# Nine of eleven pairs of rows of an FFN's last projection as block products, their weight sums in groups of three

## The chip, the cores and the metric

The kernel runs on one core of a Trainium2 chip. The metric is the device time of one execution in microseconds (us). The engines are named as in the profile: PE is TensorE (matmuls; PEld its weight loads), DVE is VectorE, ACT is ScalarE, POOL is GpSimd and SP is SyncE, which here only issues transfers. Times inside an execution are counted from the start of the profiled span.

## The reference

One layer of a streaming encoder on x of 512 tokens by 1024 features: a normalization, a combined input projection, banded attention beside a gated linear recurrence, both merged by gates and a projection, and then a gated FFN. All in float32. The part that the change touches is the last product:

```python
h = h + (g_a * ya + g_b * yb) @ w_o[l]
hn = rmsnorm(h, norm_ffn_g[l])
gu = hn @ w_ffn_in[l]
g, up = jnp.split(gu, 2, axis=-1)
h = h + (jax.nn.silu(g) * up) @ w_ffn_out[l]
return rmsnorm(h, final_norm_g)
```

`w_ffn_out` has 2816 rows and 1024 columns: 22 blocks of 128 rows, or eleven pairs of blocks, 512 KB for each half of the columns.

## The kernel before

Every float32 operand of a matmul is split into a high part (ACT rounds it by a copy, L86) and a low part (DVE subtracts, L87). One product of a 128x128 operand with 512 columns is then three matmuls, high by high, high by low and low by high (`mm3`, L78).

**Two ways to do a pair.** Let a pair be the 512 tokens by 256 inner features of the activation, times 256 rows by 1024 columns of `w_ffn_out`. A *plain* pair (`out_pair`, L1527) multiplies each of four token blocks with each of two halves of the columns, over two row blocks: 4 x 2 x 2 x 3 = 48 matmuls of 512 columns. A *block* pair cuts the activation and the weights into 2 x 2 blocks and does seven block products instead of eight (`out_block`, L1533): 7 x 2 x 3 = 42 matmuls. For that it needs sums. On the activation's side `a_first` (L1507) splits the left operand of the first products, `a_sums` (L1511) makes four sums with DVE and splits them into the right operand, and `a_second` and `a_last` (L1521, L1524) make the left and right operands of the later products. On the weights' side it needs t1 to t4, which are sums of the four blocks of the weights. The results of the seven products are added to and subtracted from the rows of `h` out of PSUM (`h_add`, L1537; `h_sum`, L1541).

**The weight sums** are made in DRAM while earlier stages run. Pairs are put in groups of `GROUP` (L206). For each group and kind SP copies a block of the weights into a buffer (`out_copy`, L222), and POOL then adds another one to it by an accumulating transfer (`out_add`, L226). All copies and sums are kept in a list each, t1 and t3 of every group first, then t2, then t4. `step` (L238) takes the next one from a list. Copies are taken one after each of the 16 attention heads, as `COPIES` says (L1166). Sums are taken after the heads in `ADDS_AT`, then one beside each of the first four products of the attention's output projection (L1186, the tiles `po_ya`), and then in the FFN's first projection, four in each unit named in `ADDS` (`fg1` and `fg2`, L1443), each after a small POOL copy that waits for a point in that unit. The product with `w_o` lies between them (its results are `o_x`, `o_y`, `o_z`).

**The order of the last projection** (from L1584). PE, DVE and ACT run in the order in which the code issues them; the planner orders only the transfers of SP and POOL there. The stages are:

- the plain loop: the plain pairs for the left half of the columns (fo0 weights); after each but the first, DVE and ACT make a left operand, one pair's sums and another left operand;
- the p stage (`p_one`, `p_two`): for each block pair one product into the banks `p_out` and one into `po_out`, both with fo0 weights. After each pair `p_then` (L1640) makes one more left operand, and after the second, fourth and sixth also one pair's sums. `two_sided` (L1609) holds the second products of the last three pairs back to the end;
- `h_sum` for `po_out`, and then the plain pairs but the last two for the right half (fo1 weights);
- the t stage (`t_one`, L1659, `t_two`): products of the right operands with t12 (t1 and t2 side by side), into `p_out` and `q_out`, held back in the same way. Before each pair, sums that are still open are made, one pair at a time; after each pair from the fifth on, one `a_second`;
- the t3b stage (L1688): two products per pair with t3 and another block, in two groups of pairs, the last one of six, each group first into `p_out` and then into `q_out`;
- the t4 stage: one product per pair for both row blocks;
- the last two plain pairs for the right half, and the final normalization and the output by pieces.

**Weights.** `weights` (L455) makes a tile and a number of further ones ahead. `out_sums` (L244) loads one of t12, t3b or t4; its high half (`high_first`, L195) goes to ACT at once, and its low half is kept back in a list until the next tile is made or the last one made is used (`low_parts`, L200):

```python
act.activation(hi, src, AF.Copy)
lows.append(lambda: dve.tensor_sub(lo, src, f(hi)))
```

There are seven tiles for split weights and five for raw ones. The left and right operands of the pairs, two tiles a pair, come from `pair_tile` (L1502): first from those tiles of the pool `sums` that are free, then from a pool of `PAIR_TILES`. The split parts of the plain pairs (`split_act`, L1428) and the t4 weights share the 13 tiles of the pool `act`.

Of the kernel before, what the change touches and what calls it, by code (L numbers as in the profile page):

```python
# [9 lines left out]
F32R = mybir.dt.float32r  # L10
# [4 lines left out]
P = 128  # L15
# [15 lines left out]
V_CW, V_CB, V_BR, V_BI, V_LAM, V_BM, V_GF = 0, 32, 40, 48, 56, 64, 80  # L31
NV = 88
CW = 256
N_PLAIN = 3
GROUP = 2
COPIES = [1] * 16
ADDS_AT = (9, 11, 13, 15)
ADDS = {"fg1": 1, "fg2": 1}
PAIR_TILES = 2 * (11 - N_PLAIN) - (4 - (N_PLAIN - 1))


@with_exitstack
def block_kernel(ctx: ExitStack, tc: tile.TileContext, x, norm_mix_g, w_in, b_merge, rel_table,
# [3 lines left out]
    pe, dve, act, pool, sp = nc.tensor, nc.vector, nc.scalar, nc.gpsimd, nc.sync  # L47

    def pool_of(name, bufs=1, side="left"):
        return tc.tile_pool(name=name, bufs=bufs, side=side, reuse_waits="tile")  # L50
# [85 lines left out]

    plain, paired = list(range(N_PLAIN)), list(range(N_PLAIN, FT // 2))

# [66 lines left out]
    t4_raw = {}  # L205
    groups = [paired[n:n + GROUP] for n in range(0, len(paired), GROUP)]  # L206
    out_t = {}
# [30 lines left out]
    def step(todo, n=1, **more):  # L238

        for _ in range(min(n, len(todo))):  # L240
            what, *of = todo.pop(0)
            what(*of, **more)
# [873 lines left out]
    def weigh(h, pp):  # L1116
        pr, e = divmod(h, 2)
        own, other = halves(e)
        if e == 0:
            oacc.append(tg_.tile([P, S], F32, tag="tg", name=f"oacc{pr}"))  # L1120
        acc = oacc[pr]
        po = mm_tile(f"o{h}")
        for kb in range(NT):
            i, lo, n = ((0, 0, 512), (1, 0, 384), (2, 0, 256), (2, 256, 128))[kb]
            st = vs[pr // 2][kb][:, pr % 2, 2 * e:2 * e + 2].rearrange("p a d -> p (a d)")
            for part in range(2):
                pe.matmul(po[:, S - n:S], st, pp[i][:, part, lo:lo + n], start=kb == 0 and part == 0, stop=kb == NT - 1 and part == 1)  # L1127
        act.activation(acc[own, :], po[other, :], AF.Copy)
        dve.tensor_add(acc[own, :], po[own, :], acc[own, :])
        if e == 1:  # L1130
            if pr % 2 == 0:
                aT_pairs.append(rnp.tile([P, 2, 2, S], F32R, tag="big", bufs=4, name=f"aT{pr}"))
            o = aT_pairs[-1][:, pr % 2]
            split(blocks(o[:, 0]), blocks(o[:, 1]), backwards(acc[:]))
            aT.append(o)
# [22 lines left out]
    with tc.manual_schedule(engines={mybir.EngineType.PE}):  # L1158
        v_all(sums)
        for h in range(HEADS):  # L1160
# [4 lines left out]
            weigh(h, pp)  # L1165
            step(copies, COPIES[h])  # L1166
            if h in ADDS_AT:
# [11 lines left out]
    for j in range(KT):  # L1179
# [11 lines left out]
        else:  # L1191
            i = j - 4
# [91 lines left out]
    acp = ctx.enter_context(pool_of("act", 13))  # L1284
# [213 lines left out]
    left, right_ = {}, {}  # L1498
    spare_tags = ["t10", "t11", "t20", "t21"][N_PLAIN - 1:]
    ohp = []  # L1500

    def pair_tile(i, name):  # L1502
        if spare_tags:
            return sums_room.tile([P, 2, 2, 256], F32R, tag=spare_tags.pop(), bufs=1, name=f"{name}{i}")
        return ohp[0].tile([P, 2, 2, 256], F32R, tag="act", bufs=PAIR_TILES, name=f"{name}{i}")

    def a_first(i):  # L1507
        o, left[i] = act2[i], pair_tile(i, "left")
        split(left[i][:, :, 0], left[i][:, :, 1], o[:, :, 0:256])

    def a_sums(i):  # L1511
        o, right_[i] = act2[i], pair_tile(i, "right")
        s = tg_.tile([P, 2, 256], F32, tag="tg", name=f"s_{i}")
        a11, a12, a21, a22 = (o[:, c, t * 256:t * 256 + 256] for t in range(2) for c in range(2))
        dve.tensor_sub(s[:, 1], a21, a22)
        dve.tensor_sub(s[:, 0], s[:, 1], a11)
        dve.tensor_sub(a11, a11, a21)
        dve.tensor_add(a12, a12, s[:, 0])
        split(right_[i][:, :, 0], right_[i][:, :, 1], s[:])
# [30 lines left out]
    def h_scale(cc, t, at=every):  # L1550

        if t not in scaled:
            scaled[t] = ohp[0].tile([P, D], F32, tag="act", bufs=PAIR_TILES, name=f"hg{t}")
        n = slice(cc * S + at.start, cc * S + at.stop)
# [202 lines left out]
```

## Time and profile before

| what | us |
|---|---|
| median of 3 runs | 846.4 (845.92 to 849.75) |
| the profiled execution, whole | 847.21 |
| its span, first to last instruction | 845.4 |
| last projection, first to last matmul | 729.89 to 839.03 |
| mean granted clock of TensorE | 0.998 of full speed |

A row of a timeline gives the start in us, the length in us, the engine, the line of the code, the operation, the tile written and the tiles read, the shape, and how many instructions are merged in it; in brackets stands how long the engine was idle before it and what ended that. A row of the view by windows gives the stretch, its length, and for each engine its busy time with the number of instructions that lie in it or reach into it, then the granted clock, the mean share in which the 16 DMA engines were busy, and GB/s. A row of the view of waits gives who waited for whom, the total in us, how often, and the longest.

### The profile page before, as it was taken

The page shows a single profiled execution, that of the slowest core. Times are in us where ns is not written, and L with a number is a line of the kernel's source. Part 1 is how long each engine was busy: PE and PEld are TensorE (multiplying, and loading weights), DVE is VectorE, ACT ScalarE, POOL GpSimd, SP SyncE. Part 2 cuts the span into 40 slices and gives each one's busy share as a digit, 9 for nine tenths or more (in the row PEclk, how much of TensorE's full clock was granted, in tenths as well). Part 3 has the DMA queues.
Part 4 walks back from the last instruction along what each step waited for, and adds up shares of the span by engine and source line. Part 5 has one row for each costly group of instructions (what it writes and reads, how often), then busy time and mean ns, then how long its engine had stood idle before and what let it go on. Part 6 is the DMA issues. An engine that isn't in the chain of part 4 may idle for free.

```text
span 845.4 us, 11956 instructions
## 1 busy us (share of the span) xinstructions
PE 836.4 (99%) x4246; PEld 708.0 (84%) x4246; DVE 658.3 (78%) x960; ACT 521.0 (62%) x862; POOL 159.6 (19%) x207
## 2 busy tenths in 40 slices
PE   9999999999999999999999999999999999999996
PEld 6988888888878888888888888888888999988885
DVE  6667779886999878877568767888777878997784
ACT  7595848773456678878544559663665465455553
POOL 3412030221040043343211000005102321300000
PEclk9999999999999999999999999999999999999999
DMA  9433486687565445548458974565955576644542
GB/s 290 163 102 116 132 298 234 215 274 248 170 203 150 137 138 145 165 141 221 91 136 215 316 293 156 154 191 167 210 193 157 147 194 179 216 154 146 160 168 99
DMA packets 107323, 153.98 MB, mean 182 GB/s; under 512 B 8216, under 2 KB 66160, under 8 KB 106752
## 3 DMA queue, kind: packets, MB, share of 16 engines
q1 hardware_dynamic: 102304, 141.32, 51.7%
q0 software_dynamic: 3728, 8.96, 6.5%
q10 hardware_dynamic: 1232, 2.95, 0.9%
q8 instruction: 33, 0.54, 0.3%
q14 instruction: 26, 0.21, 0.1%
HBM read 139.53 MB, written 30.45 MB: 201 GB/s over the span
## 4 chain that ended last, share of the span: by engine, by line
PE 95%; DVE 2%; ACT 1%; DMA 0%; issue 0%; ACTq 0%; DVEq 0%
PE fu_x L81 2%; PE fu_x L82 2%; PE fu_x L80 2%; PE o L1127 2%; PE fg_x L82 2%; PE fg_x L81 2%; PE fg_x L80 2%; PE pT L1107 2%; PE po_gb L80 2%; PE po_xr L81 2%; PE po_xr L80 2%; PE po_ga L82 2%; PE po_q L80 2%; PE po_k L80 2%; PE po_q L81 2%; PE po_ya L82 2%
## 5 line engine op out<-in xcount | busy, mean ns | idle before, releaser
L1096 POOL TENSOR_SCALAR p<-p,rl 128x128 f32<-128x128 f32 (+3 forms) x61 | 44.2, 742 | 13.6 <-DVE rl L1092 9.3
L1348 POOL TENSOR_TENSOR sg<-sg,keep_fu_x 128x512 f32<-128x512 f32 x8 | 14.5, 1817 | 159.1 <-DVE keep_fu_x L1347 159.1
L1090 DVE CUSTOM_DVE_ANT_0 p<-s,bias 128x128 f32<-128x128 f32 (+1 forms) x64 | 28.6, 486 | 13.0 <-PE s L1082 11.5
L1091 ACT ACTIVATE p<-p,m 128x128 f32<-128x128 f32 (+1 forms) x64 | 35.4, 555 | 2.3 <-DVE m L1090 2.0
L87 DVE TENSOR_TENSOR whl_fu_w<-raw_fu_w,whl_fu_w 128x1024 fp32r<-128x1024 f32 (+1 forms) x18 | 23.2, 1290 | 9.0 <-ACT whl_fu_w L86 8.9
L87 DVE TENSOR_TENSOR whl_fu_t<-t_fu,whl_fu_t 128x1024 fp32r<-128x1024 f32 (+1 forms) x18 | 24.7, 1383 | 4.9 <-ACT whl_fu_t L86 4.9
L87 DVE TENSOR_TENSOR pp<-pT,pp 128x384 fp32r<-128x384 f32 (+1 forms) x48 | 26.9, 596 | 2.0 <-ACT pp L86 1.8
L81 PE MATMUL po_xr<-xnT,whl_xr 128*128 128x512 f32 (+1 forms) x80 | 27.7, 353 | 0.0
L81 PE MATMUL po_gr<-xnT,whl_gr 128*128 128x512 f32 (+1 forms) x80 | 27.5, 347 | 0.0
L82 PE MATMUL po_gr<-xnT,whl_gr 128*128 128x512 f32 (+1 forms) x80 | 27.3, 347 | 0.0
L82 PE MATMUL po_xr<-xnT,whl_xr 128*128 128x512 f32 (+1 forms) x80 | 27.2, 346 | 0.0
L80 PE MATMUL po_gr<-xnT,whl_gr 128*128 128x512 f32 (+1 forms) x80 | 27.1, 347 | 0.0
L743 POOL MEMSET bias<- 64x64 f32 x16 | 2.4, 147 | 129.1 <-DMA bias<-ext_d 104.9
L80 PE MATMUL po_xr<-xnT,whl_xr 128*128 128x512 f32 (+1 forms) x80 | 26.3, 351 | 0.4 <-ACT xnT L654 0.4
L86 ACT ACTIVATE whl_fu_w<-raw_fu_w 128x1024 fp32r<-128x1024 f32 (+1 forms) x18 | 17.7, 986 | 13.6 <-issue 7.6
L80 PE MATMUL po_k<-xnT,whl_qk 128*128 128x512 f32 x64 | 25.5, 398 | 0.0
L80 PE MATMUL po_q<-xnT,whl_qk 128*128 128x512 f32 x64 | 25.5, 398 | 0.0
L80 PE MATMUL po_ga<-xnT,whl_ga 128*128 128x512 f32 x64 | 25.4, 397 | 0.0
L80 PE MATMUL po_gb<-xnT,whl_gb 128*128 128x512 f32 x64 | 25.2, 394 | 0.0
L82 PE MATMUL po_ga<-xnT,whl_ga 128*128 128x512 f32 x64 | 25.0, 391 | 0.1
L81 PE MATMUL po_ga<-xnT,whl_ga 128*128 128x512 f32 x64 | 25.0, 390 | 0.0
L81 PE MATMUL po_q<-xnT,whl_qk 128*128 128x512 f32 x64 | 24.9, 390 | 0.0
(689 smaller groups left out, 3086.0 us busy)
## 6 DMA issues: line engine op xcount, KB each, us to landing
raw_qk<-in_w_in_dram SPq DMA_DIRECT2D x32, 256.0 KB, 3.4
out_t<-in_w_ffn_out_dram SPq DMA_DIRECT2D x16, 512.0 KB, 5.6
raw_fu_w<-in_w_ffn_in_dram SPq DMA_DIRECT2D x16, 512.0 KB, 4.7
raw_fo<-in_w_ffn_out_dram SPq DMA_DIRECT2D x14, 512.0 KB, 4.4
raw_t<-out_t SPq DMA_DIRECT2D x24, 256.0 KB, 3.7
raw_xr<-in_w_in_dram SPq DMA_DIRECT2D x8, 512.0 KB, 5.7
raw_gr<-in_w_in_dram SPq DMA_DIRECT2D x8, 512.0 KB, 4.3
raw_ga<-in_w_in_dram SPq DMA_DIRECT2D x8, 512.0 KB, 4.3
```

What stands on the lines that cost most here:

```text
L80: pe.matmul(o, sh, mh, start=start, stop=False, skip_group_check=parts)
L81: pe.matmul(o, sh, ml, start=False, stop=False, skip_group_check=parts)
L82: pe.matmul(o, sl, mh, start=False, stop=stop, skip_group_check=parts)
L86: act.activation(hi, src, AF.Copy)
L87: dve.tensor_sub(lo, src, f(hi))
L743: pool.memset(b[64:128, 448:512], NEG)
L1090: dve.tensor_tensor_reduce(prob[qb][:], scs[qb][:, 0:w], bias[:, S - w:S], -1.0, 3e38, ALU.add, ALU.min, nmax[:, qb:qb + 1])
L1091: act.activation(prob[qb][:], prob[qb][:], AF.Exp, bias=nmax[:, qb:qb + 1], scale=-1.0, accum_out=lsum[:, qb:qb + 1])
L1096: eng.tensor_scalar(prob[qb][:], prob[qb][:], rl[:, qb:qb + 1], 1.0, ALU.mult, ALU.mult)
L1107: pe.transpose(pt[:, at * P:(at + 1) * P], prob[qb][:, kb * P:(kb + 1) * P], ident[:])
L1127: pe.matmul(po[:, S - n:S], st, pp[i][:, part, lo:lo + n], start=kb == 0 and part == 0, stop=kb == NT - 1 and part == 1)
L1348: (pool if keep and (unit != f_units[-1] or side) else dve).tensor_mul(o, o, keep_ if keep else bank)
```

## The change

`N_PLAIN` goes from 3 to 2, so that nine pairs are done as block products. The weight sums are made in three groups of three pairs (`GROUP` from 2 to 3): twelve copies and twelve accumulating transfers of 768 KB instead of sixteen and sixteen of 512 KB. `COPIES` has twelve entries of one and then four of zero, so the last four heads issue none. The list of sums is empty after four in attention, four beside `po_ya` and four in `fg1`, and `fg2` gets none. With two plain pairs no plain pair is left for the place between the p and the t stage, and the first group of the t3b stage has three pairs. The pool `sums` has one more tile free for the operands of the pairs, and one further operand tile comes from the pool `act`, so that the pool of `PAIR_TILES` keeps its 14 tiles.

```diff
-N_PLAIN = 3
-GROUP = 2
-COPIES = [1] * 16
+N_PLAIN = 2
+GROUP = 3
+COPIES = [1] * 12 + [0] * 4
 ADDS_AT = (9, 11, 13, 15)
 ADDS = {"fg1": 1, "fg2": 1}
-PAIR_TILES = 2 * (11 - N_PLAIN) - (4 - (N_PLAIN - 1))
+PAIR_TILES = 2 * (11 - N_PLAIN) - (4 - (N_PLAIN - 1)) - 1
...
     spare_tags = ["t10", "t11", "t20", "t21"][N_PLAIN - 1:]
     ohp = []
+    pair_spare = [True]
 
     def pair_tile(i, name):
         if spare_tags:
             return sums_room.tile([P, 2, 2, 256], F32R, tag=spare_tags.pop(), bufs=1, name=f"{name}{i}")
+        if pair_spare and pair_spare.pop():
+            return acp.tile([P, 2, 2, 256], F32R, tag="act", bufs=13, name=f"{name}{i}")
         return ohp[0].tile([P, 2, 2, 256], F32R, tag="act", bufs=PAIR_TILES, name=f"{name}{i}")
```

## The prediction

> **What bounds the kernel now.** First the page: its head and the busy time of the engines; then the waits of PE alone.
>
> ```profile
> span 845.4 us, 11956 instructions
> ...
> PE 836.4 (99%) x4246; PEld 708.0 (84%) x4246; DVE 658.3 (78%) x960; ACT 521.0 (62%) x862; POOL 159.6 (19%) x207
> ```
> ```profile
> PE busy L478 <- DVE eps_t L484: 1.2, 1, 1.2
> PE v_z L81 <- DVE whl_v_t L87: 0.5, 1, 0.5
> ```
>
> TensorE is the bound and hardly waits: its longest waits are 1.2 us at the start and one of 0.5 us. A matmul taken away is worth its full time, and nothing else can be gained; any new wait of PE is lost in full. So I need the length of a matmul in the last projection, and how close VectorE (DVE) and the transfers are to making PE wait. The view by windows gives both; in the second fence it is restricted to the tile of the t12 weights.
>
> ```profile
> 746.24:768.00 21.76, 21.76 (x98) 18.02 (x96) 17.27 (x29) 8.19 (x11) 0.00 (x0) 1.00 0.39 121
> 768.00:773.44 5.44, 5.44 (x26) 4.50 (x24) 5.37 (x10) 4.89 (x9) 0.00 (x0) 1.00 0.29 96
> 773.44:795.20 21.76, 21.76 (x98) 18.02 (x96) 17.39 (x25) 14.09 (x20) 0.00 (x0) 1.00 0.57 181
> ```
> ```profile
> 773.44:795.20 21.76, 21.76 (x96) 17.83 (x95) 7.02 (x6) 3.99 (x5) 1.00 0.57 181
> ```
>
> The windows are the p stage (fo0 weights on the left operands), the plain pair of the right output half, and the t stage (t12 weights on the right operands). PE is full in all; 96 matmuls in 21.76 us are 0.2267 us each, so a block of six is 1.36 us and a pair's two blocks 2.72 us. DVE is at 17 of 21.76 us, but in the short window between them at 5.37 of 5.44: there it catches up. Now DVE's timeline in these stages. This stretch has its order written out by hand for PE, DVE and ACT, and every DVE row shown stands in that order.
>
> ```profile
> 763.44 1.37 DVE L1539 TENSOR_TENSOR h<-p_out,h 128x512 f32<-128x512 f32 x2 [1.07 <-PE p_out L82]
> 767.52 1.37 DVE L1544 TENSOR_TENSOR h<-po_out,h 128x512 f32<-128x512 f32 x2 [2.71 <-PE po_out L82]
> 768.80 1.22 DVE L198 TENSOR_TENSOR whl_t<-raw_t,whl_t 128x1024 fp32r<-128x1024 f32 x1
> ...
> 772.18 3.49 DVE L198 TENSOR_TENSOR whl_t<-raw_t,whl_t 128x1024 fp32r<-128x1024 f32 x3
> 775.59 0.42 DVE L1515 TENSOR_TENSOR s<-act 128x256 f32<-128x256 f32 x1
> ...
> 777.78 1.22 DVE L198 TENSOR_TENSOR whl_t<-raw_t,whl_t 128x1024 fp32r<-128x1024 f32 x1
> ...
> 785.19 1.22 DVE L198 TENSOR_TENSOR whl_t<-raw_t,whl_t 128x1024 fp32r<-128x1024 f32 x1
> 790.64 1.37 DVE L1539 TENSOR_TENSOR h<-h,p_out 128x512 f32<-128x512 f32 x2 [4.23 <-PE p_out L82]
> 791.92 2.35 DVE L198 TENSOR_TENSOR whl_t3b<-raw_t3b,whl_t3b 128x1024 fp32r<-128x1024 f32 x2
> 794.19 0.68 DVE L87 TENSOR_TENSOR left<-act,left 128x512 fp32r<-128x512 f32 x1
> 794.80 1.29 DVE L1539 TENSOR_TENSOR h<-q_out,h 128x512 f32<-128x512 f32 x2
> 796.00 2.49 DVE L87 TENSOR_TENSOR left<-act,left 128x512 fp32r<-128x512 f32 x4
> 798.41 7.02 DVE L198 TENSOR_TENSOR whl_t3b<-raw_t3b,whl_t3b 128x1024 fp32r<-128x1024 f32 x6
> ```
> ```profile
> 761.01 1.05 ACT L197 ACTIVATE whl_t<-raw_t 128x1024 fp32r<-128x1024 f32 x1
> ```
>
> Prices, from one start to the next: the two additions from a PSUM bank 1.28 us (767.52 to 768.80); the low half of a weight tile 1.14 (1.22 to its end); the sums of one pair's right operand with their split 2.19 (775.59 to 777.78); a left operand's low half 0.60 (796.00 to 798.41, four of them). What matters most is where the first t12 low half stands: ACT has the high half at 761.01, DVE makes the low one only at 768.80, behind the two additions that wait for PE's last p product. The p stage ends at 768.00, its first row half 0.68 sooner at 767.32, so DVE starts 0.20 behind the bank.
>
> **The change part by part.**
>
> Matmuls. A plain pair costs 48 (two output halves, four row blocks, six each), a block pair 42 (seven block products of six). One pair is moved over: six fewer, -1.36 us.
>
> Plain stage. The split of one plain operand between ACT and POOL goes. I count it at nothing: what ACT, POOL or DVE gain there ends in DVE's wait for PE (1.07 us before 763.44), and PE does not wait in this stage.
>
> p stage. It begins 24 matmuls (5.44 us) earlier, with two left operands ready instead of four. From there DVE has two additions (1.28), seven left operands (4.2), three sums (6.6) and four fo0 low halves (4.6): 16.7 us. PE needs 6 x 2.72 + 2 x 1.36 = 19.0 us until the last pair. No stall, 2 us of cover; without the cover what is missing is lost one for one.
>
> t stage. Here the change takes the cover away. Before, 24 plain matmuls (5.44 us) lay between p and t, and three sums were left for the t stage. After, nothing lies between, since no plain pair is left for that place, and five sums are left: nine pairs, one done in the plain loop and three in the p stage. I count from the end of the first row half of the last p product. DVE: 0.20 wait, 1.28 for the additions, five sums 10.95, seven t12 low halves 7.98, four left operands 2.40, the last low half 1.22, 0.06 to PE: 24.1 us. PE up to the matmul that reads the last low half: 0.68, six pairs 16.32, two blocks 2.72, one matmul 0.23: 19.95 us. The difference, **4.1 us, is a stall**. It falls in parts: at the second pair 0.20 + 1.28 + 2.19 + 1.22 + 0.06 = 4.95 against 0.68 + 2.72 + 0.23 = 3.63, so 1.3; the rest at the last two pairs. The same sum for before: the last low half is done at 785.19 + 1.22 = 786.41, and the last pair begins at 773.44 + 5 x 2.72 + 2 x 1.36 = 789.76, with 3.3 us to spare.
>
> t3b stage. Its loop goes in a first group and a last one of six. The first group grows from two pairs to three, so the third tile is wanted after two blocks instead of four. PE from the restart to there: five matmuls 1.13, three held blocks 4.08, two blocks 2.72, one matmul 0.23: 8.16. DVE: 0.71 until the bank is done (two matmuls, the 0.20 and the 0.06), 1.28 for the additions, two low halves 2.27, one left operand 0.61, two additions 1.20, four left operands 2.41, one low half 1.22, 0.06: 9.76, less the 0.06 at the restart. **A stall of 1.5 us.** Before it had 1.0 to spare (798.41 + 1.22 against 800.64). From here on the low halves are ahead, and t4 and the end have slack.
>
> The last projection: -1.36 + 4.1 + 1.5 = +4.3 us. Bounds: -1.4 (DVE ready in time) and +5.9 (each of the four waits 0.4 longer: PE's restart shows in no row here, and the shortest wait shown is the 0.5 us one).
>
> The weight sums. Copies on the SP queue go from 16 of 512 KB to 12 of 768 KB, POOL's accumulating transfers likewise.
>
> ```profile
> out_t<-in_w_ffn_out_dram SPq DMA_DIRECT2D x16, 512.0 KB, 5.6
> ```
> ```profile
> 300.26 0.56 SPq L224 DMA_DIRECT2D out_t<-in_w_ffn_out_dram  x1
> 309.56 0.55 SPq L224 DMA_DIRECT2D out_t<-in_w_ffn_out_dram  x1
> ```
>
> In attention a copy has 9.3 us to the next; 1.5 x 5.6 = 8.4 fits. In the code each head's bias is issued ahead of its copy. I take 0 (bounds 0 and 1). The last four heads lose their copies, and the second FFN unit its four sums: no gain, PE is full there. The sums are done one unit sooner than before, far ahead of the t12 loads.
>
> The sums beside the ya and w_o products are the risk. Four stay there, each half as large again. The fences are the windows, POOL's part of the DMA view (437 to 470), PE's timeline and DVE's.
>
> ```profile
> 437.00:453.00 16.00, 16.00 (x73) 13.23 (x72) 13.51 (x23) 7.02 (x11) 2.94 (x5) 1.00 0.82 207
> 453.00:470.00 17.00, 17.00 (x77) 14.08 (x76) 15.78 (x28) 8.28 (x13) 2.41 (x3) 1.00 0.81 187
> 470.00:484.00 14.00, 13.99 (x62) 11.28 (x61) 9.43 (x15) 6.37 (x10) 0.00 (x0) 1.00 0.99 365
> ```
> ```profile
> q0 software_dynamic: 1088, 2.10, 41.0%
> ...
> out_t<-in_w_ffn_out_dram POOLq DMA_DIRECT2D x4, 512.0 KB, 7.3
> ```
> ```profile
> 478.15 0.39 PE L80 MATMUL o_z<-whl_o_t,ms 128*128 128x512 f32 x1
> ```
> ```profile
> 477.74 0.69 DVE L1240 SCALAR_TENSOR_TENSOR h<-o_x,h 128x512 f32<-128x512 f32 x1 [0.40 <-DMA h<-in_x_dram]
> 478.35 1.22 DVE L87 TENSOR_TENSOR whl_o_t<-raw_o_t,whl_o_t 128x1024 fp32r<-128x1024 f32 x1
> ```
>
> POOL's queue took 41% of 33 us (437 to 470), 3.4 us of all engines for each sum. Half as much again is 6.8 us more; free are 0.18 x 16 + 0.19 x 17 = 6.1. So the last sum runs on into 470 to 484, where the engines are at 0.99. There PE's o_z product needs this low half six matmuls after 478.15, at 479.5, and has it at 478.35 + 1.22 = 479.57: no slack, behind an addition that waits for a transfer of x. I take 1.3 us of delay, between nothing (it all fits) and 4 us (a third of the engines goes to the sum for its 1.5 x 7.3 = 11 us). The first FFN unit has the same four larger sums; I add 0.2 there (0 to 1.5).
>
> By the Trainium skill ("DMA: Bandwidth & Descriptors", section "Anatomy of one DMA — SWDGE (gpsimd) path") a transfer is about 2.0 us plus its bytes at 436 GB/s: an estimate of 3.2 us for 512 KB and 3.8 for 768 KB. The 7.3 us above do not agree; by the page the delay here would be at most 0.6 us, and the sum 0.7 lower.
>
> **Sum.** 4.3 + 1.3 + 0.2 = +5.8 us. The profiled span goes from 845.4 to 851.2. That execution took 847.21 us in all, 0.8 over the median of the runs shown, 846.4; the difference goes on the median: **852.2 us, +0.7%**.
>
> **Rivals.**
> - DVE keeps ahead (the other side: no slower). DVE idles 1.07 and 2.71 us before the two additions; if it did sums or low halves in that time, the t stall would be 0.3 us and the total 846.4 - 1.36 + 0.3 + 1.5 = 846.8. It decides if 3.8 us of the t chain are drawn ahead of the additions. Against it: 768.80 behind 767.52, with its high half ready at 762.06. Chance 0.06.
> - The stalls are there but smaller, and the larger sums cost nothing: 847.5 to 850.6. For it: the four sums fit but for 0.7 us. Chance 0.16.
> - The sums hurt more: 4 us at w_o and 1.5 in the first FFN unit give 846.4 + 4.3 + 5.5 = 856.2. For it: 0.99 and no slack. Chance 0.17.
> - PE's clock falls after a stall. The granted clock is 1.00 in every window above, but none holds a stall of 2 us. I assume that the pair after each of the two longest took twice its time: 2 x 2.72 = 5.4 us more, 857.6. Chance 0.03.
>
> The Trainium skill ("TensorE: Matmul & The Clock Gate", section "Part 1: The HAM clock gate (the "warmup" mystery)") lets the clock fall after about 3.4 us of idleness; no stall above is that long, and no trace here shows it.
>
> **How the numbers follow.** My forecast, 850.6 to 854.5, has 0.58. The range 847.5 to 857.0 leaves out the first rival and the top. A measurement can tell about 0.5% from no change, 4.2 us: slower is above 850.6. That is nearly all of the forecast, the larger sums and the clock, 0.75; same has 0.23; faster would need gains elsewhere, which PE's 99% leaves no room for, 0.02.
>
> **What would show it.** PE's waits should name the low half of whl_t at the second pair (about 1.3 us) and at the last two (together about 2.8), and that of whl_t3b at the third tile (1.5); DVE should be without a gap from the additions of po_out to the last whl_t. At w_o, PE should wait for whl_o_t. Without DVE in PE's waits my sum is wrong; with waits for raw weights, the transfers were underrated.

## The result, and the profile after

The changed kernel is slower, by about one per cent.

| | before | after |
|---|---|---|
| median of the runs, us | 847.53 (845.92 to 849.75, 6 runs) | 855.73 (852.75 to 864.87, 6 runs) |
| ratio | | 1.0106, 95% interval 1.0077 to 1.0135 |
| the profiled execution, whole, us | 847.21 | 854.04 |
| its span, us | 845.4 | 852.2 |
| first product of `po_ya`, us | 423.67 | 425.02 |
| first product of the FFN unit `fg1`, us | 586.18 | 587.76 |
| last projection, first to last matmul, us | 729.89 to 839.03: 109.14 | 731.45 to 845.53: 114.09 |

The three runs before that stand ahead of the prediction are among these six. The medians and the ranges in brackets hold every run; the ratios, here and below, leave out a run that is over 1.5% above the fastest of its kernel (865.39, 861.21 and 983.69 below).

So in the profiled execution 4.95 us of the 6.8 came in the last projection, 1.56 were there when it began, and 0.3 came behind it. First the page after, the busy time of the engines, and the waits of PE (who waited for whom; total us, times, longest).

```profile
PE 835.7 (98%) x4240; PEld 706.3 (83%) x4240; DVE 663.5 (78%) x969; ACT 521.7 (61%) x867; POOL 150.1 (18%) x198
```
```profile
PE p_out L81 <- DVE whl_t L198: 3.7, 3, 1.9
PE p_out L81 <- DVE whl_t3b L198: 1.4, 1, 1.4
PE pt_mix_0t L652 <- DVE xs_mix L632: 1.3, 2, 1.2
PE busy L478 <- DVE eps_t L484: 1.2, 1, 1.2
PE v_x L81 <- DVE whl_v_w L87: 0.9, 2, 0.6
PE s L1081 <- DVE m L1090: 0.5, 1, 0.5
...
PE o_z L82 <- DVE ms L87: 0.2, 1, 0.2
```

There are the six matmuls fewer (4246 to 4240), and there are the waits: DVE's low halves of `whl_t` three times and of `whl_t3b` once. The 1.3 us at `pt_mix_0t` (0.2 before) cost almost nothing: the matmuls on an idle operand ahead of it (`busy`) end about a microsecond sooner here, and the first product of `po_xr` starts at 9.24 us instead of 9.03. DVE's timeline over the same stretch as before shows the chain (start, length, then the instruction; in brackets the idle time before it):

```profile
762.27 1.37 DVE L1542 TENSOR_TENSOR h<-p_out,h 128x512 f32<-128x512 f32 x2 [1.13 <-PE p_out L82]
766.35 1.37 DVE L1547 TENSOR_TENSOR h<-po_out,h 128x512 f32<-128x512 f32 x2 [2.71 <-PE po_out L82]
767.89 0.42 DVE L1518 TENSOR_TENSOR s<-act 128x256 f32<-128x256 f32 x1 [0.17 <-ACT oj L1549]
...
770.09 3.49 DVE L198 TENSOR_TENSOR whl_t<-raw_t,whl_t 128x1024 fp32r<-128x1024 f32 x3
...
786.87 2.49 DVE L87 TENSOR_TENSOR left<-act,left 128x512 fp32r<-128x512 f32 x4
789.28 1.22 DVE L198 TENSOR_TENSOR whl_t<-raw_t,whl_t 128x1024 fp32r<-128x1024 f32 x1
791.32 1.38 DVE L1542 TENSOR_TENSOR h<-h,p_out 128x512 f32<-128x512 f32 x2 [0.83 <-PE p_out L82]
792.63 2.35 DVE L198 TENSOR_TENSOR whl_t3b<-raw_t3b,whl_t3b 128x1024 fp32r<-128x1024 f32 x2
```

Behind the 0.17 us at 767.89 and up to 790.50 no row of this timeline has an idle time in brackets: DVE works without a gap and PE runs up against it. The last low half of t12 ends at 790.50; before it ended at 786.41 and 3.3 us ahead of its reader. DVE's idle 2.71 us stands ahead of the two additions, where it helps nobody. PE's own timeline at the first of the waits shows its price:

```profile
769.55 0.39 PE L80 MATMUL p_out<-whl_t,right 128*128 128x512 f32 x1
771.37 0.50 PE L81 MATMUL p_out<-whl_t,right 128*128 128x512 f32 x1 [1.43 <-DVE whl_t L198]
771.70 0.39 PE L82 MATMUL p_out<-whl_t,right 128*128 128x512 f32 x1
771.93 0.40 PE L80 MATMUL p_out<-whl_t,right 128*128 128x512 f32 x1
```

From one start to the next are 1.82 us instead of 0.23, a stall of 1.6; and the matmul behind the wait takes 0.33 to the next start, 0.1 more than the others. By the same reading the four stalls are 1.58, 0.54, 2.05 and 1.54 us, with four restarts of 0.1.

Of the 1.56 us ahead of the last projection 0.2 are there at the first matmul of `po_xr`, some 1.1 come in the v stage (0.9 at v_x and 0.5 at s, less the 0.5 at v_z of before) and 0.2 at w_o. In the v stage the raw weights land later, by the DMA view (KB, median us to landing) of before and then of after:

```profile
raw_v_w<-in_w_in_dram SPq DMA_DIRECT2D x12, 256.0 KB, 4.0
```
```profile
raw_v_w<-in_w_in_dram SPq DMA_DIRECT2D x12, 256.0 KB, 5.5
```

The first two of the twelve copies are issued at 232 and 243 us, beside the v products, though in the code they come after the first two attention heads. That they make PE wait is not shown: in two executions below (the sums ahead of the additions, and the changed kernel again) these weights took 5.7 and 5.4 us and PE did not wait for them.

### The profile page after: what moved, and what is told of

It is laid out like the page before. It is cut to its first block, busy times and chain, and to the rows that moved or that the text cites. A ratio compares the mean times of both kernels' runs of the same rounds, so it can differ in the third digit from the quotient of the medians.

```text
span 852.2 us, 11954 instructions
## 1 busy us (share of the span) xinstructions
PE 835.7 (98%) x4240; PEld 706.3 (83%) x4240; DVE 663.5 (78%) x969; ACT 521.7 (61%) x867; POOL 150.1 (18%) x198
## 4 chain that ended last, share of the span: by engine, by line
PE 80%; DVE 8%; ACT 5%; DMA 4%; issue 2%; SPq 0%; ACTq 0%; DVEq 0%
PE fu_x L82 2%; PE fu_x L81 2%; PE fu_x L80 2%; PE o L1127 2%; PE fg_x L82 2%; PE fg_x L80 2%; PE fg_x L81 2%; PE pT L1107 2%; PE po_ga L82 2%; PE po_ya L80 2%; PE po_ya L81 2%; PE po_ya L82 2%; PE po_ga L80 2%; PE p_out L81 2%; PE po_ga L81 2%
## 5 line engine op out<-in xcount | busy, mean ns | idle before, releaser
L1096 POOL TENSOR_SCALAR p<-p,rl 128x128 f32<-128x128 f32 (+3 forms) x61 | 40.4, 677 | 13.0 <-DVE rl L1092 8.6
L80 PE MATMUL po_q<-xnT,whl_qk 128*128 128x512 f32 x64 | 25.5, 398 | 0.0
L86 ACT ACTIVATE whl_fu_t<-t_fu 128x1024 fp32r<-128x1024 f32 (+1 forms) x18 | 17.5, 985 | 12.3 <-PE fu_x L82 9.2
```

The costliest lines, as they stand in the source:

```text
L80: pe.matmul(o, sh, mh, start=start, stop=False, skip_group_check=parts)
L1096: eng.tensor_scalar(prob[qb][:], prob[qb][:], rl[:, qb:qb + 1], 1.0, ALU.mult, ALU.mult)
```

## The experiments

The theory under test: (1) the last projection loses its 5 us because DVE, behind the additions of `po_out`, has five sums and eight low halves to do before PE may go on; (2) the rest is the larger transfers for the weight sums. The rival to (1) was that the weights themselves come late; the rival to (2), that the transfers are hidden and the runs scatter for another reason. Each ratio stands against the kernel before on the same chip.

**The groups alone, without the ninth pair.** The kernel before with only

```diff
-GROUP = 2
-COPIES = [1] * 16
+GROUP = 3
+COPIES = [1] * 12 + [0] * 4
```

> The kernel before (three plain pairs) with the weight sums alone changed: groups of three, twelve copies and twelve sums of up to 768 KB. The DVE theory (the loss is made in the t and t3b stages, where DVE lost its cover): the last projection is untouched, so PE has no wait there, and the time is that of before within 0.3%. The transfer theory (the loss is made by the larger copies and sums beside the v, w_o and fg1 products, and differs from run to run with them): 0.4 to 0.8% slower than before, with a wider spread of the runs, and PE waits of together 1 to 4 us ahead of the last projection, by its low halves whl_v_w or whl_o_t.

Measured: 848.63 us (847.58 to 852.17) against 846.41, ratio 1.0029 (1.0017 to 1.0041). Its last projection takes 109.14 us, to the hundredth that of before, and PE's waits are

```profile
PE busy L478 <- DVE eps_t L484: 1.2, 1, 1.2
PE o_z L82 <- DVE ms L87: 1.1, 1, 1.1
```

So transfers of up to 768 KB instead of 512, with the same bytes in all, cost some 2.2 us by themselves, and none of it in the last projection.

**Nine pairs, but groups of two.** The changed kernel with

```diff
-GROUP = 3
-COPIES = [1] * 12 + [0] * 4
+GROUP = 2
+COPIES = [2] * 4 + [1] * 12
-ADDS = {"fg1": 1, "fg2": 1}
+ADDS = {"fg1": 1, "fg2": 2}
```

> The changed kernel with nine block pairs, but the weight sums in groups of two and one of one, as transfers of 512 KB and 256 KB (two copies after each of the first four heads, eight sums in the second FFN unit). The DVE theory: the four waits of the changed kernel in the last projection stay as they are, 5.5 to 6 us together, and the time is 0.4 to 0.7% over before. The transfer theory: the time falls to within 0.3% of before, and the spread of the runs with it.

Measured: 860.59 us (857.38 to 863.44), ratio 1.0159 (1.0139 to 1.0179).

```profile
PE p_out L81 <- DVE whl_t L198: 3.7, 3, 1.9
PE fg_x L82 <- DVE whl_fg_t L87: 2.9, 1, 2.9
PE p_out L81 <- DVE whl_t3b L198: 1.4, 1, 1.4
```

The waits in the last projection are the same to a tenth (114.04 us in all), whatever the transfers look like: they don't depend on them. The total was a miss for both theories: smaller transfers, but twenty of each kind instead of twelve and eight sums in one FFN unit, cost more than the larger ones did in the first measurement (1.0106) and no less than in the second below (1.0130), with a wait of 2.9 us for that unit's weights. As size, number and place of the sums all differ, this run doesn't tell which of them costs.

**DVE's order: the sums ahead of the additions.** In the changed kernel the additions of `po_out` are moved behind the t stage:

```diff
         two_sided(p_one, p_two, p_then)
-        for a in range(2):
-            h_sum(0, a, po[a][:], 0)
-        po = [bank("mm", f"po_out1_{t}") for t in range(NT)]
...
             a_last(i)
+        for a in range(2):
+            h_sum(0, a, po[a][:], 0)
+        po = [bank("mm", f"po_out1_{t}") for t in range(NT)]
```

> The changed kernel with one step moved: the two additions of po_out to h (h_sum) no longer stand ahead of the t stage in DVE's order but behind the last a_last, so DVE needn't wait for the held p products. The DVE theory, by the same sum as in the prediction: DVE starts the t chain 4.1 us sooner, the waits on whl_t fall from 4.2 us to about 0.1, that on whl_t3b stays at 1.5, and the time is 4 us below that of the changed kernel. If that chain isn't what sets the time, nothing changes. The transfer theory: same as the changed kernel within 0.2%.

Measured: 848.45 us (846.91 to 851.51), ratio 1.0025 (1.0015 to 1.0034); the last projection takes 109.71 us.

```profile
PE p_out L81 <- DVE whl_t3b L198: 1.4, 1, 1.4
PE busy L478 <- DVE eps_t L484: 1.2, 1, 1.2
```
```profile
759.53 1.37 DVE L1542 TENSOR_TENSOR h<-p_out,h 128x512 f32<-128x512 f32 x2 [1.39 <-PE p_out L82]
760.82 0.42 DVE L1518 TENSOR_TENSOR s<-act 128x256 f32<-128x256 f32 x1
```

All three waits for `whl_t` are gone from the view, since DVE now makes sums where it idled for 2.71 us (its timeline, second fence; PE's own timeline still has 0.1 us at the last low half, as expected); that for `whl_t3b`, which has another cause, stays. Theory (1) is shown for the t stage: the loads, the matmuls and DVE's work are the same, only its order differs. The time fell by more than the 4 us expected: the two profiled executions lie 7.1 us apart (854.04 and 846.91), 4.4 in the last projection and 2.7 ahead of it, where the edit changes nothing.

**And the third tile.** On top of it the low half of the third t3b tile instead of the second is made ahead of the additions at the end of the t stage:

```diff
-                weights(f"t3b_{paired[1]}", 0)
+                weights(f"t3b_{paired[2]}", 0)
```

> As the run with h_sum moved, and the low half of the third t3b tile is made together with the first two, ahead of the additions of q_out. The DVE theory: the wait on whl_t3b goes too, no wait over 0.3 us is left in the last projection, its length is 107.5 us against 108.9 before, and the time is 5.5 us below that of the changed kernel. The transfer theory: same as the changed kernel within 0.2%; what is left over before in this run is then what the transfers cost.

Measured: 847.34 us (845.1 to 852.68), ratio 1.0016 (1.0000 to 1.0032). The last projection takes 108.04 us, 1.1 less than before.

```profile
PE busy L478 <- DVE eps_t L484: 1.2, 1, 1.2
PE o_z L82 <- DVE ms L87: 0.8, 1, 0.8
PE v_x L81 <- DVE whl_v_w L87: 0.6, 1, 0.6
```

No wait that the view lists is left in the last projection, and theory (1) is shown for the t3b stage too. The stage saves 1.1 us, yet the kernel isn't faster than before: about 2 us are lost ahead of it, as in the groups-only run.

**The changed kernel again,** on the chip of the next three.

> The changed kernel unchanged, beside the kernel before and the three others on one chip. If its time is the sum of the waits that its trace shows (5.7 us in the last projection plus four restarts of about 0.1, 1.1 in the v stage, 0.2 at w_o, less 1.4 of matmuls, so 5.8 to 6.8 us over before), its ratio is 1.007 to 1.008 (852 to 853 us). If something that the one profiled execution didn't show is paid in most runs (in the first measurement the runs' median stood 1.7 us over the profiled execution), it is 1.009 to 1.011 again (854.5 to 856).

Measured: 859.25 us (852.25 to 865.39), ratio 1.0130 (1.0099 to 1.0161). The runs do stand above the sum of the first trace's waits, and this execution, 859.22 us itself, shows with what:

```profile
PE p_out L81 <- DVE whl_t L198: 3.7, 3, 1.9
PE fg_x L81 <- DVE whl_fg_t L87: 2.7, 1, 2.7
PE o_z L82 <- DVE ms L87: 1.8, 1, 1.8
PE p_out L81 <- DVE whl_t3b L198: 1.4, 1, 1.4
...
PE fu_x L81 <- DVE whl_fu_w L87: 1.1, 1, 1.1
```

The waits in the last projection are those of the first trace. New are 2.7 and 1.1 us in the FFN's second pair of units (`fg1` and `fu1`) and 1.8 at w_o instead of 0.2: the same program, but the transfers took longer. From 586 to 612 us, the DMA view of the first execution and then of this one:

```profile
out_t<-out_t POOLq DMA_DIRECT2D x4, 768.0 KB, 8.2
...
raw_fg_w<-in_w_ffn_in_dram SPq DMA_DIRECT2D x3, 512.0 KB, 5.8
```
```profile
out_t<-out_t POOLq DMA_DIRECT2D x4, 768.0 KB, 9.3
...
raw_fg_w<-in_w_ffn_in_dram SPq DMA_DIRECT2D x3, 512.0 KB, 8.1
```

In the kernel before, with sums of 512 KB, these weights took 4.8 us there. At w_o DVE's timeline has

```profile
474.90 0.69 DVE L1240 SCALAR_TENSOR_TENSOR h<-o_x,h 128x512 f32<-128x512 f32 x1 [3.11 <-DMA h<-in_x_dram]
...
480.96 0.68 DVE L87 TENSOR_TENSOR ms<-za,ms 128x512 fp32r<-128x512 f32 x1
```

with 3.11 us of waiting for a transfer of x, 2.15 before, and the low half of `ms`, for which PE then waits, stands behind it in DVE's order.

And the last projection took 115.64 us instead of 114.09. The view by windows, cut into stretches of 3.41 us (length, PE, PEld, DVE, ACT, POOL, granted clock, DMA share, GB/s), of this execution and then of the first one:

```profile
791.16:794.57 3.41, 1.53 (x8) 0.92 (x7) 3.00 (x5) 3.41 (x6) 0.00 (x0) 1.00 0.46 154
794.57:797.98 3.41, 3.41 (x10) 2.63 (x9) 2.20 (x3) 3.41 (x6) 0.00 (x0) 0.50 0.51 159
797.98:801.40 3.42, 3.42 (x17) 2.81 (x16) 2.77 (x5) 1.26 (x2) 0.00 (x0) 1.00 0.50 164
```
```profile
785.77:789.18 3.41, 2.51 (x10) 1.42 (x8) 3.41 (x6) 3.41 (x7) 0.00 (x0) 1.00 0.50 156
789.18:792.59 3.41, 2.04 (x9) 1.70 (x10) 2.57 (x4) 3.41 (x7) 0.00 (x0) 1.00 0.50 140
792.59:796.00 3.41, 3.41 (x17) 2.83 (x16) 3.41 (x5) 2.87 (x4) 0.00 (x0) 1.00 0.52 168
```

It is the same stall of 2.05 us, the one before the last pair of the t stage. In the second execution it lies whole in one stretch, in which PE is busy for only 1.53 us; the clock is then 0.50 for the next stretch, with 10 matmuls in it instead of 17, and 1.55 us are lost. In the first it is cut by the end of a stretch, no stretch has less than 2.04 us of work, and the clock stays at 1.00. Where the stretches end differs from execution to execution.

**The copies two heads later.** From here three variants of the version without waits in the last projection (the third-tile one). First

```diff
-COPIES = [1] * 12 + [0] * 4
+COPIES = [0] * 2 + [1] * 12 + [0] * 2
```

> The version without a wait in the last projection (sums ahead of the additions, third tile's low half earlier), with the twelve copies after heads 2 to 13 instead of 0 to 11, so that none lies beside the v products. If the first two copies delay the raw v weights and with them PE: the waits of v_x and s (0.6 to 1.4 us) go, the first pT product is at 280.5 to 281.1 instead of 281.45, and the time falls by 0.5 to 1.2 us against the version with the copies at heads 0 to 11 (847.34, 1.0016), to a ratio of 1.000 to 1.001. If the copies have nothing to do with these waits: they stay, and the time is the same within 0.3 us.

Measured: 847.66 us (845.66 to 861.21), ratio 1.0010 (0.9997 to 1.0023). The waits of v_x and s are gone, the first pT product is at 280.35, and the DMA view has

```profile
raw_v_w<-in_w_in_dram SPq DMA_DIRECT2D x12, 256.0 KB, 3.3
```

instead of 5.5. The ratio is 0.0006 below that of the third-tile version, 0.5 us and well inside both intervals, so the price of these copies was not confirmed in the time; and in two executions with the copies where they were (the sums ahead of the additions, and the changed kernel again) pT began at 279.69 and 280.08 without these waits. They are paid in some executions only. What this profile shows in their place is one wait of 3.6 us for `whl_fg_t` in `fg1`, where the clock fell as well.

**No sums beside ya.** The four sums there go into `fg2`:

```diff
-        step(adds, j < 8 - len(ADDS_AT), after=f(mT[j][:, 0, 0:1]))
+        step(adds, 0, after=f(mT[j][:, 0, 0:1]))
```

> The same version, with the copies at heads 0 to 11, and the four sums beside the ya products moved into the FFN's second unit (four in attention, four in each of two units). If the larger sums beside ya and w_o delay the w_o weights: the wait of o_z on ms (0.8 us) goes and the stretch from the first po_ya to the first pt_ffn product is 76.3 us or less (77.1 to 77.6 in the versions with the sums there, 76.75 before), worth 0.5 to 1.0 us against 847.34 (ratio 1.0005 to 1.001). If the wait is the x transfers' and not the sums', nothing there changes. Moved into the second unit the sums may cost there: 0 to 0.5 us by the kernel before, which had four of 512 KB in it, up to 2.9 by the version in groups of two with eight there.

Measured: 854.81 us (849.08 to 861.59), ratio 1.0092 (1.0056 to 1.0127). The wait of o_z is gone, as theory (2) has it, and the stretch from the first `po_ya` to the first `pt_ffn` product is 76.5 us (77.4 in the third-tile run, 76.3 expected). This alone shows little, since with the sums there the run before this one also had no such wait, and 76.25 us. But the price in the FFN was put far too low:

```profile
PE fg_x L82 <- DVE whl_fg_t L87: 3.3, 1, 3.3
PE fu_x L81 <- DVE whl_fu_w L87: 2.0, 1, 2.0
```

**Both edits.**

> Both edits together. If the transfers' cost is those two places and nothing else, what is left is six matmuls fewer (1.36 us) and 0 to 0.5 us in the second unit: a ratio of 0.9985 to 0.9995 (845.2 to 846), faster than before by about 1 us. If the transfers cost something in every place where they lie, moving them only moves the cost, and the ratio stays at 1.001 to 1.002.

Measured: 856.68 us (851.1 to 983.69), ratio 1.0082 (1.0057 to 1.0108), with waits of 7.4 us in all for `whl_fg_t` (the run of 983.69 stands alone: its mean granted clock is 0.80, where the other five have 0.992 to 0.996, and nothing here shows why). A gain was expected if the two places were all; the other theory, that moving the transfers moves the cost, was nearer and still too low.

**The sums spread.** Six in attention, two each beside ya, in `fg1` and in `fu1`, so that in the FFN no two lie together:

```diff
-ADDS_AT = (9, 11, 13, 15)
-ADDS = {"fg1": 1, "fg2": 1}
+ADDS_AT = (9, 11, 12, 13, 14, 15)
+ADDS = {"fg1": 1, "fu1": 1}
...
-        if unit in ADDS and kind in after:
+        if unit in ADDS and kind in ("w11", "t2"):
```

> The version without a wait in the last projection, with the sums of 768 KB spread: six in attention (after heads 9 and 11 to 15), two beside ya, two in fg1 (beside w11 and t2) and two in fu1, so that in the FFN no two of them lie together. If the waits of 2.7 to 3.6 us for weights of fg1 in two of the profiled executions, and the fall of the clock behind them, come from sums that lie together: no such wait, runs within 1.5 us of each other like those of before, and a median of 845.5 to 847 us (ratio 0.999 to 1.000: six matmuls fewer, less the v stage's 1.1). If sums of 768 KB cost what they do wherever they lie: the waits only move, to attention or to fu1, and the median is 847.3 or more with a spread of 5 us or more.

Measured: 848.76 us (847.89 to 850.87), ratio 1.0023 (1.0012 to 1.0035). Half of it came: the runs lie within 3 us (1.5 expected), none as far off as the 861.21 above, and PE has no wait for the FFN's weights. The median is no better; the wait is now at w_o:

```profile
PE o_z L82 <- DVE ms L87: 1.7, 1, 1.7
```

The same with the first two copies moved behind heads 2 and 3 (`COPIES = [0, 0, 2, 2] + [1] * 8 + [0] * 4`):

> The same with the first two copies moved behind heads 2 and 3 (two copies each), out of the v stage. If these two cost the v stage its 1.1 us and have cover in attention: 0.8 to 1.2 us less than the version before it, 844.8 to 846 us, faster than the kernel before by 1.4 us (ratio 0.998). If attention has no cover for them: waits of PE on the attention's probabilities in its first heads, and no gain.

Measured: 849.65 us (847.36 to 851.91), ratio 1.0022 (1.0007 to 1.0037): no gain. PE has no wait on the probabilities, which the second theory named, nor for `whl_v_w`; it waits 2.8 us at w_o, now in `o_y`, and the clock fell there.

**The changed kernel with its sums spread,** its last projection as it is:

> The changed kernel with nothing but its sums spread as above, so the waits in the last projection stay (1.6, 0.5, 2.1 and 1.5 us) while the transfers are quieter. If these waits are the change's cost: the last projection takes 114.1 us (109.1 before), or 115.6 where the 2.1 us wait falls into one stretch of 3.41 us with the one of 0.5 and the granted clock is 0.50 for the next 3.41; the runs lie in two groups, 5 and 6.5 us over the version with the sums spread and no waits, 850.5 to 853.5 us (ratio 1.005 to 1.008), and the runs above 856 of the changed kernel are gone. If those runs came of something else, they stay.

Measured: 856.18 us (851.67 to 857.28), ratio 1.0101 (1.0077 to 1.0124). The last projection is 114.08 us, with the same waits as ever; that part held. The rest didn't: three of the six runs are above 856, and in the profiled one PE waits in attention,

```profile
PE pT L1107 <- POOL p L1096: 2.4, 3, 1.9
```

with the clock at 0.50 from 393.49 to 396.90. Spreading the sums did not make these transfers quiet.

**No sums at all.** The version of the later copies, with none of the accumulating transfers issued; the sums of the weights are left out of the computation:

```diff
-        tc.keep_in_program_order(pool.dma_start(out=out_t[kind, g[0]][0][:], in_=what, accum_op=ALU.add, max_dma_last_dim=4096))
+        del what
```

> The version without a wait in the last projection and with the copies after heads 2 to 13, but with none of the twelve accumulating transfers issued: the sums t1 to t4 of the weights are left out, so the blocks that PE multiplies are the plain copies; every matmul, copy and load stays. If the accumulating transfers cause the waits for weights in the FFN, at w_o and the spread of the runs: none of these waits, runs within 1.5 us of each other, the first fg1 product at 585.1 or less, the last projection at 108.0 us, and a median of 844.0 to 845.2 us (ratio 0.997 to 0.998), 2.5 to 3.7 us below the same version with them (847.66). If the copies or the loads of the larger groups do it, the waits of 2.7 to 3.6 us for fg1's weights and runs above 849 us stay.

Measured: 845.31 us (844.86 to 847.53) against 847.36, ratio 0.9981 (0.9972 to 0.9990). PE's waits are down to two, both in the first stages:

```profile
PE busy L478 <- DVE eps_t L484: 1.2, 1, 1.2
PE po_xr L80 <- ACT xnT L654: 0.4, 2, 0.2
```

From 586 to 612 us the raw weights land in 4.1 us instead of 5.8 and 8.1:

```profile
raw_fg_w<-in_w_ffn_in_dram SPq DMA_DIRECT2D x3, 512.0 KB, 4.1
```

All waits for FFN weights and at w_o went with the twelve transfers, and the median fell by 2.35 us (847.66 to 845.31, or 2.2 with the run of 861.21 left out), a little less than the 2.5 to 3.7 expected; the copies and the loads of the larger groups, which stayed, cause none in this execution. The spread of 2.7 us is wider than the 1.5 expected, but the runs above 849 are gone. That shows which of the transfers cost, as theory (2) had it. It takes away all of the sums, though, and not only their growth: that the larger size costs rests on the groups-only run. It is no version to use; of those that compute the whole layer none was faster than the kernel before. The nearest, with both of DVE's waits mended, lie 0.10 and 0.16% above it, and the first of these can't be told from no change.

## Why the prediction was right or wrong

- **Size and range.** Forecast 852.2 us and +5.8; the medians are 855.73 and, a second time, 859.25, or +8.2 and +11.9. The first lies above the forecast's 854.5 and inside the range (up to 857.0), the second above both. The profiled execution is +6.8. Direction and mechanism held, the size was too small.
- **Matmuls, -1.36.** Six fewer. Without a wait the last projection is 1.10 shorter (109.14 to 108.04); of the 0.26 that are missing, 0.22 are in PE's timeline of that run: at the last low half (784.52 + 1.22 = 785.74) two starts lie 0.34 us apart instead of 0.23, too short for the view of waits.
- **Plain and p stage, no stall.** Right: PE waits for nothing there.
- **t stage, 4.1 us: 1.3 at the second pair, 2.8 at the last two.** Measured 1.58, then 0.54 and 2.05: 4.2. DVE's order is shown as its cause. DVE had one gap of 0.17 us, where none was expected.
- **t3b stage, 1.5 us at the third tile.** Measured 1.54, and shown by taking it away.
- **PE's restart,** which only the upper bound held: 0.1 us each, four times, 0.4 in all. With it the last projection is +4.95, against +4.3, inside its bounds.
- **Copies, 0 (0 to 1).** Mis-placed: it argued from the spacing in attention, but the first two copies lie in the v stage. In the first trace about 1.1 us were lost there, in others nothing; that the copies did it is not shown.
- **w_o, 1.3 (0 to 4).** 0.2 and 1.8 us in two executions of the changed kernel, gone without sums: the right mechanism (DVE behind an addition that waits for x), and as uncertain as its bounds said. The tile was another: PE waits for the low half of `ms`, which DVE makes behind that addition too, and not for `whl_o_t`.
- **First FFN unit with sums (`fg1`), 0.2 (0 to 1.5).** This step failed. It was 0 in the first trace and 3.8 with `fu1` in the second. The working for w_o, where the engines' share was summed and found short, was not made for this unit, although its windows before were already at 0.9 with sums of 512 KB (the runs without sums show what the weights take alone: 4.1 us).
- **The clock, rival at 5.4 us and 0.03.** Mis-sized both ways: cheaper and far more common. It fell in seven of the fourteen profiled executions, over all versions; of the four that have the t stage's stalls it fell there in one, where it cost 1.55 us. It was given little because no stall was over 3.4 us; see below.
- **The other rivals.** DVE did not keep ahead: it took no sum ahead of the additions until the code was changed so. The sums' rival (856.2) lies nearest to the first median, and its two places were right, but its prices were not: it put 4 us at w_o and 1.5 in the FFN, and two executions have 0.2 and 1.8 there, 0 and 3.8 here. That its sum fits so well is luck.
- **What the typical run adds to the first trace.** 855.73 is 1.7 over the profiled 854.04. The FFN's waits and the clock, each present in some executions and absent in that one, are shown to be of this size; how much of the 1.7 each holds wasn't measured. The mean granted clock of each run, which is on record, says that the clock has a part in it: in the profiled executions it was 0.997 to 0.999 without a fall, 0.996 or 0.997 with one low stretch, and 0.993 and 0.992 with two and three. The two slowest of the first six runs, 859.14 and 864.87, have 0.995; in the second measurement the three slowest have 0.993, 0.992 and 0.995. But 853.72 us came with 0.996, so the clock is not all of it.

## What to carry to other kernels

Where an engine that feeds the bound one works in a fixed order, count its work from the last point at which it waits, not by its share of the span: DVE at 78% cost 4.2 us because its idle 2.71 us stood ahead of the wrong instruction, and moving three lines took the stall away. A background transfer that was hidden at one size need not be hidden at one and a half, and moving it only moves the place; sum the shares for every stretch in which it lies, and look at several executions before a place is called free. A stall of the tensor engine can cost more than its length, since its clock may fall behind it.

## What the runs showed of the hardware

**The clock can fall after a stall of 2 us.** The granted clock in these traces changes only at the ends of stretches of 3.41 us, whose place differs from execution to execution. Over all profiled executions, outside the first and the last microseconds, it fell at the end of seven stretches, in which PE was busy for 0.63 to 1.53 us of the 3.41 (by PE's timelines); after a stretch at full clock with 1.55 us or more it never fell. It stayed low for one stretch in five of these executions and for two and three in the others. With 1.88 us of idle time the stall in the t stage reaches that only where it lies whole in a stretch, an estimate of (3.41 - 1.88) / 3.41 = 45% of the executions. The Trainium skill ("TensorE: Matmul & The Clock Gate", section "Part 1: The HAM clock gate (the "warmup" mystery)") puts the window at 3413 ns and calls it free-running, which agrees; but its table lets the clock fall after an idle window of about that length, and that does not: 1.88 us of idle time were enough.

**Accumulating transfers.** Those of 768 KB landed in 7.1 to 10.9 us in the first trace of the changed kernel, the 512 KB ones of before in 5.2 to 9.2; and 512 KB loads of weights beside them (`raw_fg_w`, 586 to 612 us) took 5.8 and 8.1 us in the median in two executions of the changed kernel, and 4.1 in the run without sums.
